# Loads of a block as 512 KB column halves, one with each store, in a kernel of batched q·kT scores

## The chip, the cores and the metric

The kernel runs on one core of one Trainium2 chip. The metric is device time in microseconds (us) of one execution. Several executions of each kernel are timed in rounds beside the kernel before on the same chip. A ratio given here is the mean time of one kernel's fast runs over the mean of the other's fast runs of the same rounds, so it is not quite the ratio of the medians that are quoted.

## The reference

```python
q, k: float32 (8, 12, 1024, 64)
out = np.einsum('bhid,bhjd->bhij', q, k)      # float32 (8, 12, 1024, 1024)
```

That is 96 heads. Each reads 0.5 MB and writes 4 MB: 50.33 MB are read and 402.65 MB written, so the output is eight ninths of the traffic.

## The kernel before

Blocks of up to eight heads are loaded, cast to float16 by GpSimd, transposed by VectorE, multiplied by TensorE, evicted from PSUM by ScalarE into one of three 4 MB output buffers, and stored by one DMA per head.

```python
def load(self, n, eng):                    # 1 MB: one of q, k for half a block
    half, x = divmod(n, 2)
    ...
    pin(eng.dma_start(
        out=self.raw[half][:, x],                              # 128 x 2048 f32
        in_=src.rearrange("(p r) d -> p (r d)", p=P)))         # 8 KB per partition
...
# in scores(): four rounds u of 4 matmuls into PSUM, one eviction each, then
pin(nc.sync.dma_start(                     # 4 MB, 32 KB per partition
    out=of[self.first + n].rearrange("(p t) j -> p (t j)", p=P),
    in_=o_sb.rearrange("p t j -> p (t j)")))
...
for n in range(3):                         # ahead of the first store
    next_load((nc.sync, nc.scalar)[n % 2])
...
h = b.first + n                            # the head's number, 0 to 95
loads = 1 if h < 5 else {2: 2, 3: 1, 4: 1}.get(h % 8, 0)
side[1] = side.get(1, []) + [lambda: next_load(nc.scalar)] * loads
b.scores(n, side)
```

## Time and profile before

| what | before |
|---|---|
| time, first 3 runs | median 1068.19 us (1065.44 to 1069.33) |
| span of the first trace | 1065.8 us |
| busiest compute engine | TensorE, 66% of the span |
| DMA | 453.26 MB at a mean of 425 GB/s, share 9 in tenths in nearly all slices |
| stores | 96 of 4 MB, on SyncE's queue |
| loads after the start | 44 of 1 MB, 8 KB packets, nearly all on ScalarE's queue |

The lines of the profile that carry this stand in the prediction. The way to read them is the DMA row first (nothing else is near its limit), then the rate, and then where the rate falls short: among loads, and in the last 12 us.

### The profile page before, as it was taken

The page shows a single profiled execution, that of the slowest core. Times are in us where ns is not written, and L with a number is a line of the kernel's source. Part 1 is how long each engine was busy: PE and PEld are TensorE (multiplying, and loading weights), DVE is VectorE, ACT ScalarE, POOL GpSimd, SP SyncE. Part 2 cuts the span into 40 slices and gives each one's busy share as a digit, 9 for nine tenths or more (in the row PEclk, how much of TensorE's full clock was granted, in tenths as well). Part 3 has the DMA queues.
Part 4 walks back from the last instruction along what each step waited for, and adds up shares of the span by engine and source line. Part 5 has one row for each costly group of instructions (what it writes and reads, how often), then busy time and mean ns, then how long its engine had stood idle before and what let it go on. Part 6 is the DMA issues. An engine that isn't in the chain of part 4 may idle for free.

```text
span 1065.8 us, 4231 instructions
## 1 busy us (share of the span) xinstructions
PE 700.8 (66%) x1568; PEld 240.7 (23%) x1568; DVE 428.6 (40%) x57; ACT 694.3 (65%) x384; POOL 354.0 (33%) x206
## 2 busy tenths in 40 slices
PE   6686756756765675675675667567567667777770
PEld 2232212212222221221222222122122222222220
DVE  4768922900940670290094067029109406700000
ACT  2687657656765765666675677576667657777771
POOL 7769055036206505502620650550261064000000
DMA  9999999999999999999999999999999999999997
GB/s 384 440 430 434 421 427 439 427 429 427 434 422 433 433 431 421 435 427 424 434 433 413 433 431 418 422 434 423 426 432 432 428 430 432 432 433 433 432 430 313
DMA packets 21909, 453.26 MB, mean 425 GB/s; under 512 B 2432, under 2 KB 2432, under 8 KB 3968
## 3 DMA queue, kind: packets, MB, share of 16 engines
q1 hardware_dynamic: 14976, 406.85, 89.2%
q10 hardware_dynamic: 6912, 46.14, 10.4%
q8 instruction: 12, 0.20, 0.1%
q14 instruction: 9, 0.07, 0.0%
HBM read 50.33 MB, written 402.65 MB: 425 GB/s over the span
## 4 chain that ended last, share of the span: by engine, by line
DMA 70%; ACT 17%; PE 7%; DVE 1%; POOL 1%; issue 1%; ACTq 0%; SPq 0%; POOLq 0%
DMA out_dram<-o_sb 70%; ACT o_sb L166 17%; PE ps L155 7%; POOL half_sb L111 1%; DVE kT L128 0%; DMA early<-in_q_dram 0%; DVE o_sb L162 0%; DVE kT L139 0%; DVE o_sb L164 0%; PE ps L136 0%; ACT o_sb L161 0%; DVE qT L139 0%; ACTq L166 0%; POOL half_sb L93 0%; SPq L74 0%
## 5 line engine op out<-in xcount | busy, mean ns | idle before, releaser
L155 PE MATMUL ps<-kT,qT 64*128 64x512 f16 x1536 | 696.9, 617 | 333.6 <-ACT o_sb L166 328.2
L166 ACT COPY o_sb<-ps 128x2048 f32<-128x2048 f32 x379 | 689.0, 1868 | 335.5 <-DMA out_dram<-o_sb 302.2
L111 POOL CAST half_sb<-x_sb 32x2048 f16<-32x2048 f32 x176 | 332.1, 1887 | 531.6 <-DMA x_sb<-in_k_dram 507.1
L155 PEld LDWEIGHTS <-qT 64*128 64x128 f16 x1536 | 237.4, 157 | 791.2 <-issue 788.3
L128 DVE STREAM_TRANSPOSE qT<-half_sb 128x2048 f16<-128x2048 f16 (+1 forms) x24 | 214.2, 8926 | 477.8 <-POOL half_sb L111 477.8
L128 DVE STREAM_TRANSPOSE kT<-half_sb 128x2048 f16<-128x2048 f16 (+1 forms) x24 | 216.2, 9009 | 0.0
L111 POOL CAST half_sb<-early 32x1024 f16<-32x1024 f32 x16 | 16.5, 1033 | 2.6 <-DMA early<-in_k_dram 1.9
L136 PE MATMUL ps<-ident,half_sb 128*128 128x128 f16 x32 | 3.9, 309 | 6.7 <-POOL half_sb L93 6.2
L161 ACT COPY o_sb<-ps 128x1024 f32<-128x1024 f32 x4 | 4.0, 1012 | 5.5 <-PE ps L155 5.5
L162 DVE COPY o_sb<-ps 128x1024 f32<-128x1024 f32 x4 | 4.9, 1224 | 5.2 <-ACT o_sb L161 5.2
L161 ACT ACT_TABLE_LOAD x1 | 1.3, 1283 | 7.7 <-DMA early<-in_k_dram 7.7
L93 POOL CAST half_sb<-early 128x512 f16<-128x512 f32 x8 | 4.7, 613 | 3.4 <-DMA early<-in_q_dram 3.2
L139 DVE COPY qT<-ps 128x1024 f16<-128x1024 f16 x2 | 2.4, 1219 | 7.3 <-PE ps L136 7.3
L136 PEld LDWEIGHTS <-half_sb 128*128 128x128 f16 x32 | 3.3, 142 | 8.3 <-POOL half_sb L93 6.2
L139 DVE COPY kT<-ps 128x1024 f16<-128x1024 f16 x2 | 2.4, 1218 | 3.8 <-PE ps L136 3.8
L164 DVE COPY o_sb<-ps 128x2048 f32<-128x2048 f32 x1 | 2.3, 2292 | 2.0 <-PE ps L155 2.0
masks.py:199 POOL TENSOR_SCALAR_AFFINE_SELECT ident<-ident 128x128 f16<-128x128 f16 x1 | 0.3, 292 | 0.1
masks.py:197 POOL MEMSET ident<- 128x128 f16 x1 | 0.2, 204 | 0.3 <-POOLq L275 0.3
L275 POOL MEMSET const-float32-0.0<- 128x1 f32 x1 | 0.1, 98 | 0.2 <-issue 0.2
L275 POOL MEMSET const-bfloat16-1.0<- 128x1 bf16 x1 | 0.1, 100 | 0.0
L275 POOL MEMSET const-uint8-127<- 128x1 uint8 x1 | 0.1, 100 | 0.0
L275 POOL MEMSET const-float32-1.0<- 128x1 f32 x1 | 0.1, 98 | 0.0
## 6 DMA issues: line engine op xcount, KB each, us to landing
out_dram<-o_sb SPq DMA_DIRECT2D x96, 4096.0 KB, 23.2
x_sb<-in_k_dram ACTq DMA_DIRECT2D x22, 1024.0 KB, 29.6
x_sb<-in_q_dram ACTq DMA_DIRECT2D x20, 1024.0 KB, 18.6
x_sb<-in_q_dram SPq DMA_DIRECT2D x2, 1024.0 KB, 13.0
early<-in_k_dram ACTq DMA_DIRECT2D x4, 256.0 KB, 5.1
early<-in_q_dram SPq DMA_DIRECT2D x4, 256.0 KB, 4.7
early<-in_q_dram SPq DMA_DIRECT2D x2, 512.0 KB, 7.2
early<-in_k_dram ACTq DMA_DIRECT2D x2, 512.0 KB, 7.6
```

Source lines behind the costliest of these rows:

```text
L93: nc.gpsimd.tensor_copy(out=self.halves[x][:, :, half], in_=self.raw[half][:, x].rearrange("p (r d) -> p r d", d=D),)
L111: nc.gpsimd.tensor_copy(out=dst[:, :, b % 2], in_=raw[32 * b : 32 * b + 32, :, :, h],)
L128: pin(nc.vector.transpose(out=dst, in_=src))
L136: pin(nc.tensor.transpose(t_ps[:, t], self.halves[x][:, t], ident))
L139: pin(nc.vector.tensor_copy(out=dst, in_=src))
L155: nc.tensor.matmul(ps[:, tt, js], qT[cs, g, 2 * u + tt], kT[cs, g, js])
L161: pin(nc.scalar.copy(out=dst[:, 0], in_=ps[:, 0]))
L162: pin(nc.vector.tensor_copy(out=dst[:, 1], in_=ps[:, 1]))
L164: pin(nc.vector.tensor_copy(out=dst, in_=ps))
L166: pin(nc.scalar.copy(out=dst, in_=ps))
L275: nc = _bacc.Bacc("TRN2", target_bir_lowering=False, num_devices=1)
```

## The change

The loads are to be spread evenly over the stores, so that no burst of loads holds a few stores up. Six 1 MB loads go ahead of the stores; after that, each load is cut into two column halves of 4 KB per partition, and one half is issued after each head from the fourth on.

```diff
-        def load(self, n, eng):
+        def load(self, n, part, parts, eng):
...
+            size = self.elems // parts
+            cols = slice(part * size, (part + 1) * size)
...
-                    out=self.raw[half][:, x],
-                    in_=src.rearrange("(p r) d -> p (r d)", p=P),
+                    out=self.raw[half][:, x, cols],
+                    in_=src.rearrange("(p r) d -> p (r d)", p=P)[:, cols],
...
+    stream = [s + (0, 1) for s in stream[:6]] + [
+        s + (part, 2) for s in stream[6:] for part in range(2)
+    ]
...
-    for n in range(3):
+    for n in range(6):
         next_load((nc.sync, nc.scalar)[n % 2])
...
-            h = b.first + n
-            loads = 1 if h < 5 else {2: 2, 3: 1, 4: 1}.get(h % 8, 0)
-            side[1] = side.get(1, []) + [lambda: next_load(nc.scalar)] * loads
             b.scores(n, side)
+            if b.first + n > 2:
+                next_load(nc.scalar)
```

More of the change, by code (lines that the diff above doesn't have):

```diff
@@ L193 @@
         for n in range(4):
-            b.load(n, (nc.sync, nc.scalar)[n % 2])
+            b.load(n, 0, 1, (nc.sync, nc.scalar)[n % 2])
     stream = [(b, n) for b in blocks[3:] for n in range(4)]
+    stream = [s + (0, 1) for s in stream[:6]] + [
+        s + (part, 2) for s in stream[6:] for part in range(2)
+    ]
     def next_load(eng):
         if stream:
-            b, n = stream.pop(0)
-            b.load(n, eng)
-    for n in range(3):
+            b, n, part, parts = stream.pop(0)
+            b.load(n, part, parts, eng)
+    for n in range(6):
         next_load((nc.sync, nc.scalar)[n % 2])
@@ L219, in to_half @@
                 return
-            if any(sb is b and n // 2 == half for sb, n in stream):
+            if any(sb is b and n // 2 == half for sb, n, _, _ in stream):
                 return
```

## The prediction

> **What bounds the kernel now.** I read the slices of the page first, then the queues, the chain of waits, the table of stretches (busy time by window), and last the packet records of the trace.
>
> ```profile
> DMA  9999999999999999999999999999999999999997
> GB/s 384 440 430 434 421 427 439 427 429 427 434 422 433 433 431 421 435 427 424 434 433 413 433 431 418 422 434 423 426 432 432 428 430 432 432 433 433 432 430 313
> DMA packets 21909, 453.26 MB, mean 425 GB/s; under 512 B 2432, under 2 KB 2432, under 8 KB 3968
> ...
> q1 hardware_dynamic: 14976, 406.85, 89.2%
> q10 hardware_dynamic: 6912, 46.14, 10.4%
> ```
>
> The 16 DMA engines are at nine tenths or more in every slice but the last, while no compute engine is above 66%. q1 is the SyncE queue (nearly all stores), q10 the ScalarE queue (nearly all loads). Together they hold the engines for 99.6% of the span, so the kernel is a stream of bytes through full DMA engines.
>
> ```profile
> DMA out_dram<-o_sb 70%; ACT o_sb L166 17%; PE ps L155 7%; POOL half_sb L111 1%; DVE kT L128 0%; DMA early<-in_q_dram 0%; DVE o_sb L162 0%; DVE kT L139 0%; DVE o_sb L164 0%; PE ps L136 0%; ACT o_sb L161 0%; DVE qT L139 0%; ACTq L166 0%; POOL half_sb L93 0%; SPq L74 0%
> ```
>
> The chain says the same from the other side: a store lands, its output buffer comes free, four evictions fill it (about 7.5 us), the next store goes out. Its 24% on ScalarE and TensorE is not time to be won: there are three output buffers, so while one is being refilled two stores are queued. In the store-only stretch a link of the chain is 29.05 us (a landing wait of 21.47 us plus the refill) for three stores, 9.68 us each.
>
> ```profile
> 100.00:860.00 760.00, 496.17 (x1095) 169.32 (x1094) 326.45 (x36) 496.81 (x274) 256.69 (x138) 1.00 1.00 428
> 900.00:1040.00 140.00, 104.26 (x231) 35.69 (x231) 24.64 (x3) 105.84 (x59) 0.00 (x0) 1.00 1.00 433
> 1040.00:1054.00 14.00, 1.03 (x3) 0.14 (x1) 0.00 (x0) 2.94 (x2) 0.00 (x0) 1.00 1.00 431
> 1054.00:1065.80 11.80, 0.00 (x0) 0.00 (x0) 0.00 (x0) 0.00 (x0) 0.00 (x0) 1.00 0.38 165
> ```
>
> The last two columns are DMA share and GB/s. With loads among the stores the stream runs at 428 GB/s, with stores alone at 433; and for the last 11.8 us the share is 0.38, because the 16 engines do not finish together. The completion records of the last store spread over 8.6 us: ten engines are done about 7 to 8.6 us before the last one, six lag. In the store-only stretch this spread stays at 8.5 us; it grew, from 0.4 us at the start, while loads were in flight. All the change can win is of this kind: some 9 us.
>
> The packet records give the sum that the whole argument rests on. Median durations on an engine: a 32 KB store packet 1213 ns, an 8 KB load packet 309 ns, 4 KB 164 ns (159 ns on the line through 2 KB and 8 KB), 2 KB 84 ns, a completion 9 ns. Per engine that is 96 x 8 x 1.213 = 931.6 us of stores, 44 x 8 x 0.309 = 108.8 us of 1 MB loads, 5.2 + 5.4 us of early loads, 152 x 0.009 = 1.4 us of completions: 1052.4 us. Data starts to flow about 2 us into the span, and after the last packet some 2 us remain. That makes about 1057 us; the span is 1065.8. The missing 9 us are what the slowest engine lost: store packets that took up to 0.5 us longer than 1213 ns. In 2 us bins of the trace this excess is nearly all where load packets flow.
>
> **What the Trainium skill says.** "DMA: Bandwidth & Descriptors", section Bandwidth (Measured), gives as a rule to batch DMAs to at least 1 MiB. Taken alone, 512 KB loads would break it. The trace does not support applying it here: what a single DMA pays in latency is hidden, since two stores are always queued behind it. The same page, "Queues, rings and completion order", says each engine goes round-robin between queues at packet granularity. The trace agrees: between 130 and 165 us, in a burst of loads, the records hold 362 store packets and 366 load packets, one for one, and q10 has 20.0% of the time, about 309/(1213+309). "Why small descriptors are slow" on that page names a fixed overhead of about 3 cycles per packet. The trace has an overhead of some 8 ns: 32 KB in 1213 ns is 27.0 B/ns, 8 KB in 309 ns is 26.5, 2 KB in 84 ns is 24.4. "HBM Reference", Specifications, has about 425 GB/s for a core streaming alone, bounded by its 16 engines; the page's mean is 425. There is no faster rate to move to.
>
> **The change part by part.** The instructions of TensorE, VectorE and GpSimd stay in the same order and count. Three things change.
>
> *Size.* Six loads stay whole (48 packets per engine); the other 38 become 76 halves. Bytes are the same. Per engine 38 x 8 packets of 309 ns (93.9 us) become 76 x 8 of 159 to 164 ns (96.7 to 99.7 us): +2.8 to +5.8 us. Then 38 more completions at 9 ns: +0.3 us. This lies on the path, since the engines are never free. I take +4 us.
>
> *Issue.* 37 more load issues on ScalarE's queue (79 against 42 of x_sb, and 3 instead of 2 on SyncE) at 0.33 us are 12 us in all, beside idle time of ScalarE (335.5 us before its evictions). Off the path: 0.
>
> *Timing.* Before, four 1 MB loads go out at heads 2, 2, 3 and 4 of each eight, and their bytes occupy about half of the time. Now one half goes out after every store from the fourth on. By the round-robin, a half (8 packets per engine) takes exactly as long as a store (8 packets per engine): 8 x (1.213 + 0.16) = 11.0 us, the period at which it is issued. So the load queue is nearly always busy yet cannot back up. The burst of stores at 12 us and the calm at 9.7 become an even 11 us. For a full queue this is the same number of bytes: 0 by itself.
>
> Does it turn into a wait? The last half of a block's loads goes out after head 14 for a block that starts at head 24. Landing takes about 14 us behind queued stores plus 11 to 22 us (the 1 MB loads on this queue take a median of 18.6 and 29.6 us), say 3 heads; half a block's casts 8 x 1.887 = 15.1 us, 1.5 heads; four transposes at 9 us, 36 us, 3.3 heads: ready by head 22. A margin of 2 heads, over 20 us. A load also waits for its input tile to be cast; that is about 6 heads earlier. And it waits for the load four before it to have landed (the completion semaphores rotate), issued 44 us earlier. No new stall in the steady part. At the start 6 MB of whole loads go ahead of the stores instead of 3, but the engines are full from 3 us on either way.
>
> Sum: 1068.2 + 4 = 1072 if the loss of the slowest engine stays at 9 us.
>
> **The rivals.** (a) *The loss follows the number of switches between store and load packets.* These double where loads are halved (304 to 608 per engine), so the 9 us could become up to 17: 1080. For it: the loss exists only where loads flow. Against it: it comes in runs of extra 0.3 us on some packets, not as a constant on each. (b) *The loss follows load bytes.* Binned by load density, the mean excess per MB is flat (0.20, 0.18, 0.17 us per MB from thin to dense bins): then nothing changes, 1072. I lean to this. (c) *The even stream cuts the loss*, because engines that run ahead never see a dense burst, or because shorter load packets hold a store up by 0.15 instead of 0.3 us. At best 6 of the 9 us are won against the 4 us paid: 1066. For it: an extra of about 0.3 us on a store packet is close to the length of one 8 KB load packet. (d) *A load blocks ScalarE's queue*, as once in the trace before (ScalarE waits 7.6 us for GpSimd at the first reuse of an input tile). If it recurred, two queued stores would cover up to some 10 us of it: nothing lost unless it is longer.
>
> **Range and chances.** I weigh (b) at half, (a) and (c) at a quarter each; (a) probably in part only. That centres near 1071 us, with 1064 to 1079 for 8 in 10. A gain over 2% needs under 1047 us, which is below the 1057 us that the packets alone take: 0.01. A loss over 2% needs above 1089.6 us, more than doubled loss plus a real stall: 0.02. Within 2%: 0.97.
>
> **What would show it.** DMA share at 9 throughout; 4 KB packets with a median near 160 ns; 76 x 128 = 9728 of them; the store-only end at 433 GB/s again. The mean rate of the mixed stretch tells the rivals apart: about 427 GB/s under (b), 423 or less under (a), 430 or more under (c), with the share in the last 12 us lower or higher as the spread of the engines is larger or smaller. Wrong would be: waits of ScalarE on x_sb loads of more than 10 us, GpSimd's casts ending so late that TensorE waits for transposes, or slices under nine tenths, which would make it slower than I say.

## The result, and the profile after

The changed kernel took 1067.09 us (6 runs, 1066.89 to 1067.20), the kernel before 1065.68 us on the same rounds (6 runs, 1064.53 to 1069.33): ratio 1.0007, with a 95% interval from 0.999 to 1.0024. The class, no change beyond 2%, and the range hold. The size does not: 1071 over 1068.19 was a forecast of 1.0026.

The DMA rows and the two main queues of the changed kernel:

```profile
DMA  9999999999999999999999999999999999999996
GB/s 381 433 430 432 429 433 432 432 429 432 431 426 435 430 428 431 431 430 430 431 429 431 432 429 428 432 431 429 430 431 429 430 429 433 431 432 428 431 433 273
DMA packets 27382, 453.28 MB, mean 425 GB/s; under 512 B 3040, under 2 KB 3040, under 8 KB 14304
...
q1 hardware_dynamic: 15120, 407.90, 89.0%
q10 hardware_dynamic: 12240, 45.09, 10.4%
```

The DMA engines are as full as before and the mean rate is the same 425 GB/s. The slices between are steadier (426 to 435, where they ran from 413 to 440). There are 5473 more packets; q10, with fewer bytes than before (one load moved to SyncE's queue), has the same share of the time.

The chain that ended last in the changed kernel:

```profile
DMA out_dram<-o_sb 70%; ACT o_sb L169 17%; PE ps L158 7%; POOL half_sb L114 1%; DMA early<-in_k_dram 1%; DVE kT L131 0%; DVE o_sb L165 0%; DVE o_sb L167 0%; ACT o_sb L164 0%; ACT L164 0%; ACTq L169 0%; DVE kT L142 0%; PE ps L139 0%; ACTq L77 0%; POOLq L114 0%
```

Two of ScalarE's waits there (total us, times, longest us):

```profile
ACT o_sb L169 <- DMA out_dram<-o_sb: 303.9, 90, 4.2
...
ACT o_sb L169 <- POOL half_sb L114: 3.9, 1, 3.9
```

It is the same chain. ScalarE waits for landed stores as long in total as before (303.9 against 302.2 us), in evener pieces (longest 4.2 against 6.5 us). The only wait for GpSimd is one of 3.9 us at the first reuse of an input tile. So no load blocks ScalarE's queue.

The stretches of the changed kernel (the last two columns are DMA share and GB/s):

```profile
100.00:860.00 760.00, 498.99 (x1101) 170.24 (x1100) 325.13 (x36) 500.30 (x276) 265.21 (x141) 1.00 1.01 430
900.00:1040.00 140.00, 104.72 (x232) 35.78 (x231) 36.23 (x4) 104.70 (x58) 10.79 (x6) 1.00 1.00 431
1040.00:1054.00 14.00, 0.51 (x2) 0.00 (x0) 0.00 (x0) 2.41 (x2) 0.00 (x0) 1.00 0.98 421
1054.00:1065.30 11.30, 0.00 (x0) 0.00 (x0) 0.00 (x0) 0.00 (x0) 0.00 (x0) 1.00 0.18 76
```

The mixed stretch runs at 430 GB/s instead of 428, although it has smaller packets. And the end is different in kind: in the last 11.3 us the share is 0.18, where it was 0.38. The completion records of the last store say who is still at work: one engine, with the next one 3.4 us ahead of it and the rest 4.0 to 10.6 us. In the first trace of before, five more engines had ended within 2 us of the last. The packets are as forecast: 4 KB packets have a median of 159 ns, and there are 9728 more of them. The store-only stretch ran at 431 GB/s, not at the 433 that the prediction expected again.

### The profile page after: what moved, and what is told of

Its sections match the earlier page's. It is cut to its first block, busy times and chain, and to the rows that moved or that the text cites. A ratio compares the mean times of both kernels' runs of the same rounds, so it can differ in the third digit from the quotient of the medians.

```text
span 1065.3 us, 4306 instructions
## 1 busy us (share of the span) xinstructions
PE 700.8 (66%) x1568; PEld 240.8 (23%) x1568; DVE 427.0 (40%) x57; ACT 694.5 (65%) x384; POOL 354.5 (33%) x206
## 3 DMA queue, kind: packets, MB, share of 16 engines
q10 hardware_dynamic: 12240, 45.09, 10.4%
## 4 chain that ended last, share of the span: by engine, by line
DMA 71%; ACT 17%; PE 7%; POOL 1%; DVE 1%; issue 1%; ACTq 0%; POOLq 0%
DMA out_dram<-o_sb 70%; ACT o_sb L169 17%; PE ps L158 7%; POOL half_sb L114 1%; DMA early<-in_k_dram 1%; DVE kT L131 0%; DVE o_sb L165 0%; DVE o_sb L167 0%; ACT o_sb L164 0%; ACT L164 0%; ACTq L169 0%; DVE kT L142 0%; PE ps L139 0%; ACTq L77 0%; POOLq L114 0%
## 5 line engine op out<-in xcount | busy, mean ns | idle before, releaser
L169 ACT COPY o_sb<-ps 128x2048 f32<-128x2048 f32 x379 | 689.2, 1869 | 333.3 <-DMA out_dram<-o_sb 303.9
## 6 DMA issues: line engine op xcount, KB each, us to landing
out_dram<-o_sb SPq DMA_DIRECT2D x96, 4096.0 KB, 25.6
```

What stands on the lines that cost most here:

```text
L169: pin(nc.scalar.copy(out=dst, in_=ps))
```

## The experiments

Twelve runs in four batches. The kernel before was timed in each batch; its medians there were 1064.64, 1064.76, 1065.56 and 1064.54 us, all below the 1068.19 us from which the prediction started.

Two theories stood against each other. **A**: one DMA engine does work the others do not, and it alone sets the end. **B**: the prediction's, all engines share the end, and packets and mixing cost what the sum says.

### The changed kernel again

> The changed kernel once more, on the chip of this batch, as the base for the others. Theory A (one DMA engine carries, besides its sixteenth of the data, the 12 instruction fetches of 16 KB that TensorE needs, some 0.93 us each, 11.2 us in all, and it alone sets the end): within 0.3% of the kernel before, 1066 to 1068 us, one engine's last completion 3 us or more behind the next. Theory B (the prediction's: all engines share the end, 4 KB packets cost 4 us and the mixing loss 9 us): 1069 to 1072 us.

Measured: 1067.19 us (1067.09 to 1067.35) against 1064.64 us of before (11 runs, 1064.03 to 1065.63), ratio 1.0023 (1.0011 to 1.0035). The last engine ended 3.0 us after the next one, as theory A expected, and the time is within A's range. But the difference, 2.55 us, is also close to the 2.8 us that the prediction had between the two kernels, so this run does not decide between the theories. What moved since the first comparison is the kernel before.

### 1 MB loads, evenly spread

```diff
-    stream = [s + (0, 1) for s in stream[:6]] + [
-        s + (part, 2) for s in stream[6:] for part in range(2)
-    ]
+    stream = [s + (0, 1) for s in stream]
...
-            if b.first + n > 2:
+            if b.first + n > 2 and (b.first + n) % 2 == 0:
```

> The changed kernel with its halves put back to 1 MB loads of 8 KB packets, one with every second store: even in time, large packets. Theory A: the end is set by the engine with the fetches, so 1064 to 1068 us like the others, whatever the other engines lose. Theory B: the 3 to 4 us of packet cost go away and the bursts are short, so 1062 to 1064 us. On the stalls of store packets: if they come from 8 KB packets, the mean excess is again near 8 us per engine as in the kernel before; if from the long bursts of four loads, it is near 4 us as in the changed kernel.

Measured: 6 runs in two clusters, 1064.28 to 1064.92 us and 1072.03 to 1073.09 us. The traced run was of the first kind (span 1062.5 us), with a mean excess over the packet medians of 6.1 us per engine (the changed kernel 4.4 us, before 9.1 us in its first trace): between the two expectations. The fast cluster lies where the kernel before lies. The slow one fits neither theory, so it was run again:

> The even 1 MB loads again: half of their runs took 1064.5 and half 1072.5 us. If the slow half is drift of engines under 8 KB packets, a trace that falls into it shows the excess of store packets well above 6 us per engine, and several engines near the last one; its fast runs again at 1064.5 us.

Measured: 1065.47, 1066.14, 1067.28 and 1072.64 us. The traced run was the slow one (span 1070.9 us). Its excess was 11.3 us per engine, as expected, but only some 6 us of it are on store packets; nearly 5 us are on the load packets themselves. The several engines near the last one were not there: one engine was still last, the next 2.9 us ahead of it. The stretches of that trace:

```profile
100.00:860.00 760.00, 495.82 (x1093) 168.91 (x1092) 325.72 (x37) 494.77 (x273) 257.35 (x137) 1.00 1.00 427
900.00:1040.00 140.00, 105.56 (x234) 35.95 (x233) 36.17 (x4) 104.58 (x58) 11.15 (x6) 1.00 1.00 431
```

427 GB/s with loads in flight, 431 without: the slow kind loses its time where 8 KB load packets run beside the stores. What selects it from one execution to the next is open.

### The packet size without the timing

```diff
# the schedule of before, in groups and with three loads ahead, but from the seventh load on:
+    stream = [s + (0, 1) for s in stream[:6]] + [
+        s + (part, 2) for s in stream[6:] for part in range(2)
+    ]
...
             loads = 1 if h < 5 else {2: 2, 3: 1, 4: 1}.get(h % 8, 0)
+            if stream and stream[0][3] == 2:
+                loads *= 2
```

> The schedule of the kernel before (loads in groups of four on heads 2, 2, 3 and 4 of each eight, three loads ahead of the stores at the start), with each 1 MB load from the seventh on issued as two halves of 4 KB packets back to back. Only the packet size of the change, not its timing. If the packets are what costs: 1067 us, like the changed kernel. If the timing is what costs: 1064 to 1065 us, like the kernel before.

Measured: 1067.31 us (5 runs, 1066.44 to 1068.36) against 1064.76 us, +2.55 us, ratio 1.0021 (1.0007 to 1.0035). That is the first of the two expectations: the packets cost what the change costs, and the timing alone is worth nothing that shows, with 4 KB packets (1067.31 in groups, 1067.19 evenly) as with 8 KB (1064.7 us, and the fast cluster of the evenly spread ones). By the durations, 608 packets of 159 ns in place of 304 of 309 ns and 38 more completions of 9 ns are 3.1 us per engine. The excess in the trace of this run is some 6.5 us per engine, close to the 7.0 to 7.2 us of the kernel before in its usual executions. So small packets alone (some 6.5 us) or even timing alone (6.1 us) do little to it; only both together bring the 4.4 to 5.0 us of the changed kernel, and that does not show in the time.

### Store packets halved

```diff
-            pin(nc.sync.dma_start(out=..., in_=...))       # one store of 32 KB packets
+            for c in (slice(0, 4 * S), slice(4 * S, 8 * S)):
+                pin(nc.sync.dma_start(out=dst[:, c], in_=src[:, c]))
```

> The changed kernel with each 4 MB store issued as two column halves of 16 KB packets: 768 more store packets and 96 more completions per engine, bytes unchanged. If each packet costs some 8 ns on the path (what the durations 1213, 309 and 84 ns suggest): 768 x 8 ns + 96 x 9 ns = 7.0 us more, 1074 us. If the overhead is hidden by the next packet's start: 1067 to 1068 us.

Measured: 1075.92 us (4 runs, 1073.94 to 1079.02), 8.7 us over the changed kernel's 1067.2 us where 7.0 us were expected. The queue lines of its trace:

```profile
DMA packets 41207, 453.29 MB, mean 421 GB/s; under 512 B 4576, under 2 KB 4576, under 8 KB 15840
...
q1 hardware_dynamic: 28944, 407.91, 89.1%
```

The same bytes in 13825 more packets, and the mean falls from 425 to 421 GB/s. Less 0.9 us for the completions, that is about 10 ns for each of the 768 packets, where 8 were expected; the four runs spread over 5 us, so the 10 is rough. The overhead is not hidden by the next packet.

### More instruction fetches

```diff
                 for tt in range(2):
+                    pin(nc.tensor.matmul(ps[:, tt, :8], qT[cs, g, 2 * u + tt], kT[cs, g, :8]))
                     for j in range(2):
```

> The changed kernel with 768 tiny extra matmuls (8 columns, overwritten by the real ones; each also loads weights), 1536 TensorE instructions more, so about 6 more instruction fetches of 16 KB. TensorE has a third of its time free and the data traffic is the same. Theory A: the engine with the fetches gets 6 x 0.93 = 5.6 us more, so 1072 to 1073 us, and the last engine falls 16 us instead of 10.7 us behind the first. Theory B: 0.1 MB of 453 MB more, 0.2 us spread over all engines: 1067 us unchanged.

Measured: 1070.74 us (5 runs, 1070.03 to 1070.84), 3.55 us over the changed kernel in the same rounds, and short of A's 1072 to 1073 us. The queues of its trace:

```profile
q1 hardware_dynamic: 15120, 407.90, 88.9%
q10 hardware_dynamic: 12240, 45.09, 10.4%
q8 instruction: 18, 0.29, 0.1%
```

The data queues hold the packets of the changed kernel, one for one; q8 has 18 packets instead of 12. The last engine was 7.5 us behind the next (3.0 us without the extra fetches), but 10.4 us behind the first, not the 16 us expected. So about 0.1 MB more costs 3.55 us, which B's 0.2 us cannot explain. Divided among six fetches it would be 0.59 us each, against the 0.93 us that a fetch's record shows. The Trainium skill has the mechanism, in "Runtime: NRT & Kernel Launch", section Instruction fetch mechanics: blocks of 16 KiB, 256 instructions each, fetched by a DMA queue of the sequencer's own. The trace agrees: 1536 instructions more brought 6 packets of 16 KB more.

A control with more TensorE time and fewer fetches:

```diff
                 for tt in range(2):
+                    if tt == 0:
+                        pin(nc.tensor.matmul(ps[:, tt, :512], qT[...], kT[cs, g, :512]))
```

> A control for the run with more instruction fetches: the changed kernel with half as many extra matmuls (384, so 768 TensorE instructions and 3 fetches more) but each of full length (512 columns), so with far more TensorE time. If the fetches on one DMA engine are what counts, the slope of that run (3.5 us for 6 fetches, 0.58 us each) gives +1.8 us: 1069 us. If TensorE's time or the longer refill of an output buffer counted, it would be more than the 3.5 us of that run: 1071 us or more.

Measured: 1068.42 us (5 runs, 1068.19 to 1068.50), some 1.2 us over the 1067.19 us of the changed kernel (timed in another batch), with TensorE busy 837.3 us instead of 700.8. TensorE's time does not count. What counts came with the added instructions, at 0.4 to 0.6 us for each 256 of them, which is also one fetch. These two runs cannot tell instructions from fetches, since both were added in the same ratio.

The packet records say more, and they speak against theory A's reason. They name no engine, but on an engine each record starts 3 to 4 ns before the one ahead of it ends, so the sixteen sequences can be followed from record to record. (A check, in the second trace of the kernel before: each sequence has 750 store packets from 60 us on, one has 751, and each has 304 load packets.) Followed in this way, none of the 15 fetches after 200 us in the trace with 768 tiny matmuls, and none of the 30 in the three traces of the changed kernel, is on the engine that ends last. In the former trace they go to eight engines in turn, as far as they can be followed, and each delays its engine by some 1.3 us. After the last fetch of the changed kernel's first trace, at 1007 us, the engine that had it ends 8 us before the last one.

What sets the last engine apart is something else. Between 100 and 900 us of the changed kernel, 85% of its store packets are more than 1 ns longer than the median of 1213 ns, and the mean is some 13 ns longer; of the other engines' store packets 4% are. (These are counts in the first trace.) Over 768 store packets that is about 10 us (9.5 us in the second trace of the kernel before), and in the run with the 768 tiny matmuls it is about 13 us: some 2.5 us of the 3.55 us. So theory A is right that one engine sets the end, and wrong about why. What makes this engine's packets longer, and why more TensorE instructions make it worse, no record shows.

### One engine spared, one engine burdened

```diff
...
+            cuts = [(0, 120), (120, 128)] if self.first + n == 84 else [(0, P)]
+            for p0, p1 in cuts:
+                pin(nc.sync.dma_start(out=dst[p0:p1], in_=src[p0:p1]))
```

> The changed kernel with one store of 96 (that of head 84) cut into 120 and 8 partitions. The first part goes over 15 engines, the second over 8, so the sixteenth engine is spared 8 store packets, 9.7 us, and eight others take one more, 1.2 us. Theory A: if the engine with the fetches is the sixteenth, the end moves to the next slowest engine, 3 to 5 us earlier: 1062 to 1064 us; if it is one of the first eight, 1068 us; if another, 1067 us. Theory B: 1067 us or slightly more.

Measured: 1085.37 us (6 runs, 1075.94 to 1086.95), 18 us over the changed kernel and outside every expectation. (The trace has 7 completion records more, 15 + 8 instead of 16, as the cut intends.) The stretches ahead of that store and across it:

```profile
900.00:930.00 30.00, 22.30 (x50) 7.67 (x50) 21.49 (x3) 22.43 (x14) 12.09 (x7) 1.00 1.01 434
930.00:980.00 50.00, 22.90 (x52) 7.90 (x51) 14.77 (x2) 22.93 (x13) 0.00 (x0) 1.00 0.94 315
```

The rate falls to 315 GB/s for 50 us, and the larger part took 39.4 us to land where a whole store has a median of 25.6. The 118 store packets of that time that were slower than 1500 ns had a median of 2480 ns instead of 1213. What slowed these packets, no run shows. The experiment says nothing about the last engine.

```diff
+            if b.first + n == 80:
+                extra = consts.tile([P, 512], F32)
+                pin(nc.scalar.dma_start(out=extra[:127], in_=rows))   # 127 x 2 KB
```

> The changed kernel with one extra load of 127 rows of 2 KB at head 80. 127 partitions do not divide over several DMA engines, so by the Trainium skill it all runs on one, 127 x 84 ns = 10.7 us on that engine alone, 0.26 MB of 453. If the last engine alone sets the end: the end moves by up to 10.7 us if it is the engine that is last already (1078 us), or by 0 to 8 us if it is one that is 3 to 10.6 us ahead (1067 to 1075 us). If all engines shared the end: 0.26 MB at 433 GB/s, 0.6 us, 1068 us.

Measured: 1070.97 us (4 runs, 1070.39 to 1071.60), 3.8 us over the changed kernel, for 0.26 MB. That is inside A's range and six times B's 0.6 us. (That 127 partitions leave a transfer on one engine is from the Trainium skill, "DMA: Bandwidth & Descriptors", section Why a DMA increments its semaphore by 16 and not by 1; the records name no engine, but of the 127 packets, of 84 ns in the median, no two overlap in time, as on one engine.) All other engines then ended 1.1 to 1.7 us before the last, instead of 3.0 to 10.6. The share of 0.83 between 950 and 960 us shows engines idle there: my reading, argued and not shown, is that with three output buffers an engine can run only about one store ahead of the slowest one.

### Both kernels once more, side by side

> The changed kernel a third time, beside the kernel before. If packets of 4 KB cost 2.5 us of the end and the first comparison (ratio 1.0007) was masked by slower executions of the kernel before: 1067.2 us again within 0.3 us, and a ratio of 1.002 to 1.0025 wherever the kernel before runs at its usual 1064.5 us. If the true difference is nil: a ratio of 1.0007 or less.

> The kernel before in the same rounds, as a kernel of its own, for the spread of its executions: mostly 1064 to 1065 us, with some at 1066 to 1069 us. If it falls into the slower kind while traced, several engines end within 2 us of the last; if into the usual kind, one is last by 1.5 us or more.

Measured: changed 1067.10 us (6 runs, 1066.57 to 1067.28), ratio 1.0016 (1.0004 to 1.0028) to 11 runs of before with a median of 1064.54 us; the kernel before as a kernel of its own 1065.15 us (1064.10 to 1067.11). The ratio is between the two that I had set against each other, since three of the 11 runs of before were again at 1066.5 to 1067.4 us. Its traced run (1064.88 us) had the second engine 0.5 us before the last, where I had expected 1.5 us or more.

The kernel before had been traced once more already, in the second batch:

> The kernel before, unchanged, to have its trace from a run like those of the last batch. Theory A (the engine with TensorE's instruction fetches sets the end; the 1068 and 1069 us of its first runs were a worse drift of several engines in bursts of 8 KB loads): 1064 to 1066 us, one engine last, the excess of store packets below the 9 us per engine of the first trace. Theory B (load bursts always cost several engines 8 us): 1067 to 1069 us and six engines within 2 us of the last, as in the first trace.

Measured: 1064.36 us (5 runs, 1064.25 to 1066.71), the last engine 1.8 us behind the next, excess 7.2 us per engine. That is theory A's expectation, as far as the one last engine goes. The mixed stretch of that usual execution (span 1062.5 us):

```profile
100.00:860.00 760.00, 501.59 (x1106) 171.02 (x1105) 326.59 (x36) 502.22 (x277) 261.95 (x139) 1.00 1.00 430
```

It runs at 430 GB/s, as in the changed kernel, not at the 428 of the first trace.

Over all batches, 57 executions of the kernel before have a mean of 1065.26 us, a median of 1064.76 and a range of 1063.98 to 1069.33, with 12 above 1066 us. The 17 of the changed kernel have a mean of 1067.11 us and a range of 0.8 us. No version tried beats the kernel before.

## Why the prediction was right or wrong

**The bound: right.** DMA share and chain are unchanged. The margins for casts, transposes and buffers held: no new wait of ScalarE, VectorE's and TensorE's busy times unchanged.

**The packet term: right in kind, too large.** I took +4 us; packet size alone measured +2.55 us (group of 4 KB halves against before). I had averaged durations of 159 and 164 ns, and the lower one was right: it gives 3.1 us.

**The step that failed** is "1068.2 + 4 = 1072 if the loss of the slowest engine stays at 9 us". The 9 us were the loss of one traced execution, and 1068.19 the median of three runs of which two were of the slower kind. Counted the same way (span less 1057 us), a usual execution of before loses 5.5 us (span 1062.5). The changed kernel, whose packets alone take 3.1 us more, loses 1065.3 - 1060.1 = 5.2 us. So against the slow executions the change wins back about 3.5 us and pays 3; against the usual ones it wins nothing and pays 2.5 us. A mixture of both in the first six runs gave 1.0007; eleven usual runs gave 1.0023.

**What the 9 us were made of.** I put all of it down to mixing loads with stores. In a usual execution most of it belongs to the one engine whose store packets are some 12 to 13 ns longer, 9.5 to 10 us in all, and not only beside loads: between 900 and 940 us of the second trace of the kernel before, with stores alone, it is 12 ns. That this is more than the 5.2 to 5.5 us counted above is due to the sum of durations: an engine's records overlap by 3 to 4 ns, so its nearly 1400 packets take some 5 us less than the 1052.4 us that I had added up, and the loss is that much larger. The cause of the longer packets stays open; the instruction fetches, which theory A took for it, are on other engines. The rest, some 3 us in the first trace, I put down to drift of more engines under 8 KB load packets; that is argued from the slow runs of the even 1 MB loads, not shown.

**The rivals.** (a), a loss per switch, falls: switches doubled and the mean excess went from 9.1 (usual runs 7.0 to 7.2) to between 4.4 and 5.0 us. (c), less loss with an even stream of smaller packets, is right for that mean, but the mean is not what ends the kernel. My test for it (430 GB/s or more in the mixed stretch, a lower share at the end) came out, and yet does not prove it, since a usual run of before has 430 as well. (b) was right about the end in the usual case and wrong about the reason. (d) did not recur: the one wait of this kind was 3.9 us.

## What to carry to other kernels

When DMA engines are full from end to end, count packets as well as bytes: halving the packets of a tenth of the traffic cost 2.5 us of 1065 here, and evening out the loads returned none of it against usual runs. Read who finishes last: with one engine behind all others, what helps the fifteen does not move the end. And measure the spread of the kernel before first; three runs and one trace of it were a worse base than any term of the sum. Last, a fit of sizes is not a place: the 3.55 us fitted fetches on the last engine well, and the packet records show the fetches on others.

## What the Trainium skill lacked or had wrong

- "DMA: Bandwidth & Descriptors" has no per-packet cost for 4 to 32 KB packets of these queues. Measured: durations of 84, 159, 309 and 1213 ns for 2, 4, 8 and 32 KB, a straight line with about 8 ns per packet on top of the bytes; on the path about 10 ns (768 more store packets and 96 more completions per engine cost 8.7 us).
- "Runtime: NRT & Kernel Launch" does not say on which DMA engines the instruction fetches run, or what they cost the data there. Followed through the packet records, TensorE's fetches went to eight engines in turn, and each delayed its engine by some 1.3 us.
- "DMA: Bandwidth & Descriptors" gives how many engines a transfer of other than 128 partitions uses, but not that a store cut in this way can be slow: with one store cut at 120 partitions, 118 store packets took a median of 2480 ns instead of 1213, and the run 18 us more.
- None of the pages read has the spread of executions under mixed traffic: 1064.0 to 1069.3 us with 8 KB load packets in bursts, two clusters 8 us apart with the same packets evenly spread, 0.8 us with 4 KB packets evenly spread and 1.9 us with these in bursts.
